# Input projection of a hybrid trunk: 28 column pairs over all tokens by seven block products, in a stage ahead of the mixers

## The chip, the cores and the metric

The kernel runs on one core of a Trainium2 chip. The metric is device time in microseconds (us) of one launch. The engines are TensorE (PE; PEld is its weight load), VectorE (DVE), ScalarE (ACT), GpSimd (POOL) and SyncE (SP), which here only issues DMAs.

## What is computed

One layer over 1024 tokens of width 1024, all in float32:

```python
h = layer_norm(x)
u = h @ w_in          # columns: conformer a, g | ssm z | ssm x, B, C | dt | gate_a | gate_b
y_a = silu(layer_norm(causal_dwconv31(a * sigmoid(g)))) @ w_conv_out
xbc = silu(causal_dwconv4([x, B, C]))
y_b = rms_norm(ssd(xbc, dt) * silu(z)) @ w_ssm_out     # chunks of 128 tokens, 4 groups, 32 heads
h = layer_norm(alpha * h + (sigmoid(gate_a) * y_a + sigmoid(gate_b) * y_b) @ w_o)
h = layer_norm(alpha * h + conv_ffn(h))               # 2 x 2816 columns up, 3-tap convolution, down
```

## The kernel before

Every float32 product is made of three products of float32r operands (hi by hi, hi by lo, lo by hi: lines 166, 167 and 168 of `mm3`); ScalarE rounds an operand to its high part, VectorE subtracts to get the low one. Activations lie by channels: a tile is 128 channels by 512 tokens, and tokens are taken in two halves of 512.

The program runs half 0 through `ln_in`, `mixers`, `combine` and `out_proj`, then half 1 through the same with `out_proj_pairs` at the end, then the FFN over both halves.

- `mixers` goes over four SSD groups. For each, `column` computes one 128-column tile of `w_in` (24 products of 512 columns: 8 blocks of the contraction by 3) for B, C and four tiles of x, and `conv4` filters each with 4 taps. `z_gate` computes the group's z. `glu` computes two tiles of a and of g; `conv31` filters them with 31 taps, 30 of them as one step on VectorE each (line 420), at a priority 1500 below the rest. `ssd_group` then works through four chunks of 128 tokens. After the groups come the eight columns of gate_a. From group 2 on `ssm_out_first` multiplies the first half of the SSD output with `w_so`.
- A chunk of `ssd_group` goes round the engines: GpSimd builds `au`, TensorE multiplies it with `seg_st` (line 487), ScalarE makes the decay (495, 496), VectorE multiplies with the masked scores `cbm` (512), TensorE multiplies with `xs` (534), VectorE adds up `t` (535). Most of these tiles have one buffer, and the chunks share four PSUM banks.
- `combine` computes the eight columns of gate_b, each followed by the rest of the SSD output (`w_sp`), and beside them the LayerNorm over channels of the convolved tiles (`cc`: GpSimd sums them, TensorE spreads the mean, lines 616 to 636); then `w_co` multiplies the result `sT`.
- The FFN's up projection takes columns in 22 pairs over all tokens. With the contraction, the columns and the tokens each cut in two, a pair is a product of 2x2 blocks, done with seven block products (84 products of 512 columns) in place of eight. `ffn_blocks` makes the sums of activation blocks (b11, b21, b22, t1 to t4), `up_weights` those of weights, `up_rest` adds the products up. For the first 8 pairs (`LEAD`) `up_first` computes two of the products ahead and stores them.

The order of instructions on each engine comes from a list scheduler that builds the program by the order of the code and priorities (`tc.high_priority(offset=...)`, negative for late); each engine then runs its list strictly in order. All DMAs are issued by SyncE, in order as well. `big` is a pool of two 32 KB-per-partition buffers for `hT`, `yT` and `mixT`; `wst` and `wsp` hold three weight tiles each.

```python
                with tc.high_priority(offset=-1500):
                    conv31(pl, hh, vs)
```

Of the kernel before, what the change touches and what calls it, by code (L numbers as in the profile page):

```python
# [8 lines left out]
F32 = mybir.dt.float32  # L9
# [7 lines left out]
P = 128  # L17
# [34 lines left out]
CT_A, CT_G, CT_X, CT_B, CT_C, CT_DT, CT_GA, CT_GB = 0, 8, 16, 32, 36, 40, 41, 49  # L52
CT_N = 57
# [3 lines left out]
def kernel(  # L57
# [3 lines left out]
    wcol: bass.AP,  # L61
# [33 lines left out]
    state_stack = ExitStack()  # L95
    statep = state_stack.enter_context(pool("states", side="right"))
    upper = statep.tile([P, P], F32, name="upper")
    make_upper_triangular(nc, upper, 1.0, diag=True)
    later = statep.tile([P, P], F32, name="later")
    make_lower_triangular(nc, later, 1.0, diag=False)  # L100
    ones = statep.tile([P, P], F32, name="ones")
    V.memset(ones, 1.0)
# [22 lines left out]
    a_log = statep.tile([P, HEADS], F32, name="a_log")  # L125
    dskip = statep.tile([P, HEADS], F32, name="dskip")
    u_halo = statep.tile([P, 24, 3], F32, name="u_halo")
    G.memset(u_halo, 0.0)
    v_halo = statep.tile([P, 8, KC - 1], F32, name="v_halo")
    G.memset(v_halo, 0.0)  # L130
    states = [statep.tile([P, HALF], F32, name=f"state{g}") for g in range(GROUPS)]
    dts = [statep.tile([P, 4, HEADS], F32, name=n) for n in ("dtv", "wds")]
    edc = statep.tile([P, 3, 4, HEADS], F32, name="edc")
    seg_mv = statep.tile([P, 4, P], F32, name="seg_mv")
    seg_st = statep.tile([P, 4, P], F32R, name="seg_st")
# [10 lines left out]
    g_scr = [dram.tile([8, P, HALF], F32, name=f"g_scr{i}") for i in range(2)]  # L146
# [87 lines left out]
    def ln_in(hh):  # L234
        hT = big_tile(f"hT{hh}")
        with pool(f"lnin{hh}", side="right") as pl:
            first = hh == 0
            xts, gb = [], []
            with tc.high_priority(offset=6000):
                for t in range(4):  # L240
                    xt = pl.tile([P, D], F32, tag="x", bufs=4, name=f"x{hh}_{t}")
                    r0 = hh * HALF + t * P
                    SY.dma_start(xt, x[r0 : r0 + P, :])
                    xts.append(xt)
                    if first and t == 1:
                        gb = [row(pl, RW_ING, D, "in_g"), row(pl, RW_INB, D, "in_b")]
            if not first:
                gb = [row(pl, RW_ING, D, "in_g"), row(pl, RW_INB, D, "in_b")]
            if first:
                SY.dma_start(pc[:, :PC_N], pcol)  # L250
                SY.dma_start(a_log, prow[RW_AL : RW_AL + HEADS].partition_broadcast(P))
                SY.dma_start(dskip, prow[RW_SD : RW_SD + HEADS].partition_broadcast(P))
            for t, xt in enumerate(xts):
                with tc.high_priority(offset=(6000 - 1000 * (t // 2)) if first else 0):
                    mv, rs = ln_stats(pl, [xt], f"in{hh}_{t}")
                    ln_apply(xt, mv, rs, 0, *gb)
                    SY.dma_start(h_scr[hh][t * P : (t + 1) * P, :], xt)
                    transpose_to(hT, xt, t, 0, KD)
        return hT
# [83 lines left out]
    def column(hh, hT, ct):  # L343
        ps = bank(1)
        project(ps, weights(wcol[ct], f"c{hh}_{ct}"), hT)
        return ps

    def first_columns(hh, hT, cts):

        ws = [weights(wcol[ct], f"c{hh}_{ct}", eng=None if hh else G) for ct in cts]  # L350
        pss = [bank(1) for _ in cts]
        for q in range(2):
            ts = slice(q * 256, (q + 1) * 256)
            for w, ps in zip(ws, pss):
                for n, (i, j) in enumerate(((0, 0), (1, 0), (0, 1))):
                    for k in range(KD):
                        TE.matmul(
                            ps[:, ts],
                            w[:, i, k * P : (k + 1) * P],
                            hT[:, j, k, ts],  # L360
                            start=n == 0 and k == 0,
                            stop=n == 2 and k == KD - 1,
                        )
        return pss

    def conv4(pl, hh, ps, j):

        u = pl.tile([P, HALF + 3], F32, tag="u", bufs=3, name=f"u{hh}_{j}")
        o = pl.tile([P, HALF], F32, tag="xbc", bufs=12, name=f"xbc{hh}_{j}")
        wc = PC_SW + j * 4  # L370
        A.copy(u[:, 3:], ps)
        A.copy(u[:, :3], u_halo[:, j, :])
        A.activation(out=o, in_=ps, func=AF.Identity, scale=pc[:, wc + 3 : wc + 4])  # L373
        for k in range(3):
            V.scalar_tensor_tensor(  # L375
                out=o,
                in0=u[:, k : k + HALF],
                scalar=pc[:, wc + k : wc + k + 1],
                in1=o,
                op0=ALU.mult,  # L380
                op1=ALU.add,
            )
        if hh == 0:
            A.copy(u_halo[:, j, :], u[:, HALF : HALF + 3])
        A.activation(out=o, in_=o, func=AF.Silu, bias=pc[:, PC_SB + j : PC_SB + j + 1])
        return o

    def glu(pl, hh, hT, i):
        pa, pg = bank(1), bank(1)
        wa = weights(wcol[CT_A + i], f"ga{hh}_{i}")  # L390
        project(pa, wa, hT)
        wg = weights(wcol[CT_G + i], f"gg{hh}_{i}")
        project(pg, wg, hT)
        v = pl.tile([P, HALF + KC - 1], F32, tag="v", bufs=4, name=f"v{hh}_{i}")
        s = pl.tile([P, HALF], F32, tag="sig", name=f"sig{hh}_{i}")
        A.activation(out=s, in_=pg, func=AF.Sigmoid)
        A.copy(v[:, : KC - 1], v_halo[:, i, :])
        V.tensor_mul(v[:, KC - 1 :], pa, s)
        if hh == 0:
            A.copy(v_halo[:, i, :], v[:, HALF:])  # L400
        return v

    def conv31(pl, hh, vs):

        accs = {}
        for i, v in vs:
            wc = PC_CW + i * KC
            c = pl.tile([P, HALF], F32, tag="c", bufs=2, name=f"c{hh}_{i}")
            A.activation(  # L409
                out=c,  # L410
                in_=v[:, KC - 1 :],
                func=AF.Identity,
                scale=pc[:, wc + KC - 1 : wc + KC],
                bias=pc[:, PC_CB + i : PC_CB + i + 1],
            )
            accs[i] = c
        for k in range(KC - 1):
            for i, v in vs:
                wc = PC_CW + i * KC
                V.scalar_tensor_tensor(  # L420
                    out=accs[i],
                    in0=v[:, k : k + HALF],
                    scalar=pc[:, wc + k : wc + k + 1],
                    in1=accs[i],
                    op0=ALU.mult,
                    op1=ALU.add,
                )
        for i, _ in vs:
            SY.dma_start(c_scr[hh][i], accs[i])
# [130 lines left out]
    def mixers(hh, hT):  # L560
        pre = first_columns(hh, hT, (CT_DT, CT_B, CT_C))
        with pool(f"mixers{hh}") as pl:
            time_steps(pl, hh, pre[0])
            for g in range(GROUPS):
                BT = conv4(pl, hh, column(hh, hT, CT_B + g) if g else pre[1], 16 + g)
                CT = conv4(pl, hh, column(hh, hT, CT_C + g) if g else pre[2], 20 + g)
                xT = [
                    conv4(pl, hh, column(hh, hT, CT_X + 4 * g + i), 4 * g + i) for i in range(4)
                ]
                zs = z_gate(pl, hh, hT, g)  # L570
                vs = [(i, glu(pl, hh, hT, i)) for i in (2 * g, 2 * g + 1)]
                done = ssd_group(pl, hh, g, xT, BT, CT, zs)
                if g == 2:
                    ssm_out_first(pl, hh, yT)
                if g % 2 == 0:
                    yT = big_tile(f"yT{hh}_{g}")
                done(yT)
                with tc.high_priority(offset=-1500):
                    conv31(pl, hh, vs)
            for j in range(8):  # L580
                pg = bank(1)
                project(pg, weights(wcol[CT_GA + j], f"gt{hh}_{j}"), hT)
                ga = pl.tile([P, HALF], F32, tag="ya", bufs=2, name=f"gt{hh}_{j}")
                A.activation(out=ga, in_=pg, func=AF.Sigmoid)
                SY.dma_start(g_scr[hh][j], ga)
        return yT
# [625 lines left out]
```

## Time and profile before

| | us |
|---|---|
| median of 3 runs | 2045.84 (2041.03 to 2046.99) |
| span of the profiled execution | 2043.0 |
| TensorE busy | 1977.0 (97%) |
| VectorE busy | 1717.1 (84%) |
| ScalarE busy | 1001.3 (49%) |
| GpSimd busy | 146.8 (7%) |

The profile is of one execution. It has groups of instructions (count, busy time, mean), a table of busy time by windows of the span, the instructions in order of time, and the chain of waits that ended last. Starts and lengths are in us from the span's start. Busy TensorE is the union of records that overlap (a product's record is about 0.4 us long, and one starts every 0.225), so its share says that it was never without work, not how fast it was.

By the rows in order of time, in half 0 the products with `w_so` start at 297, gate_a at 442, gate_b at 499, `w_co` at 598 and `w_o` at 642 us; half 1 starts at 691; the FFN's first products start at 1356, its pairs at 1413, and the down projection at 1805.

### The profile page before, as it was taken

How to read it: one execution, taken by the hardware profiler on the slowest of the kernel's cores; microseconds unless marked ns; L12 is line 12 of the kernel's file. 1: busy time of each engine (PE TensorE's matmuls, PEld its weight loads, DVE VectorE, ACT ScalarE, POOL GpSimd, SP SyncE). 2: the span in 40 equal slices, each digit the busy share in tenths (PEclk: the TensorE clock that was granted, in tenths of full speed). 3: DMA queues.
4: the chain of work that ended last, by engine and by line, in shares of the span. 5: the costliest groups of instructions: out<-in, count | busy, mean ns of one | idle time of the engine just before them, and what ended most of it. 6: DMA issues, size and time to landing. Idle time of an engine off the chain costs nothing. (4 is left out here: it accounts for less than half of the span.)

```text
span 2043.0 us, 24683 instructions
## 1 busy us (share of the span) xinstructions
PE 1977.0 (97%) x9164; PEld 1627.7 (80%) x9164; DVE 1717.1 (84%) x2279; ACT 1001.3 (49%) x1431; POOL 146.8 (7%) x125
## 2 busy tenths in 40 slices
PE   7999999999999999999999999997899999989998
PEld 6888887888788888888888888876678888768886
DVE  7599999989766859999998976596888788789668
ACT  4465654556452356665454645453334445444432
POOL 2010101000400001010100040010000000000000
PEclk9999999999999999999999999998989999999999
DMA  6212223223436522222323253564343223287463
GB/s 218 93 68 89 87 93 103 98 103 114 160 124 218 200 93 73 93 78 87 117 88 109 107 175 127 207 234 174 124 138 119 95 98 117 101 316 267 145 226 109
DMA packets 99192, 275.10 MB, mean 135 GB/s; under 512 B 11264, under 2 KB 11264, under 8 KB 99072
## 3 DMA queue, kind: packets, MB, share of 16 engines
q1 hardware_dynamic: 99072, 273.52, 38.4%
q8 instruction: 72, 1.18, 0.2%
q14 instruction: 48, 0.39, 0.1%
HBM read 223.93 MB, written 49.55 MB: 134 GB/s over the span
## 5 line engine op out<-in xcount | busy, mean ns | idle before, releaser
L420 DVE SCALAR_TENSOR_TENSOR c<-v,pc,c 128x512 f32<-128x512 f32 x480 | 374.5, 803 | 7.7 <-ACT c L409 6.4
L478 POOL TENSOR_TENSOR au<-seg_mv,head_of 128x1024 fp32r<-128x1024 f32 x32 | 76.4, 2386 | 963.0 <-PE sm L487 730.1
L166 PE MATMUL acc<-hT,w_c 128*128 128x512 f32 x352 | 141.0, 401 | 0.0
L167 PE MATMUL acc<-hT,w_c 128*128 128x512 f32 x352 | 140.6, 399 | 0.0
L168 PE MATMUL acc<-hT,w_c 128*128 128x512 f32 x352 | 138.4, 393 | 0.0
L375 DVE SCALAR_TENSOR_TENSOR xbc<-u,pc,xbc 128x512 f32<-128x512 f32 x144 | 109.6, 773 | 0.7 <-ACT xbc L373 0.5
L1006 ACT CAST w_dn<-dr 128x1024 fp32r<-128x1024 f32 (+1 forms) x73 | 68.3, 944 | 76.6 <-PE sm L168 27.4
L167 PE MATMUL acc<-w_z,hT 128*128 128x512 f32 x256 | 100.8, 394 | 0.0
L166 PE MATMUL acc<-w_z,hT 128*128 128x512 f32 x256 | 100.8, 401 | 0.0
L168 PE MATMUL acc<-w_z,hT 128*128 128x512 f32 x256 | 100.7, 396 | 0.0
L154 ACT CAST w_c<-st_c 128x1024 fp32r<-128x1024 f32 x50 | 52.6, 1051 | 86.9 <-PE acc L168 66.2
L1007 DVE TENSOR_TENSOR w_dn<-dr,w_dn 128x1024 fp32r<-128x1024 f32 (+1 forms) x73 | 78.6, 1086 | 9.3 <-ACT w_dn L1006 9.1
L167 PEld LDWEIGHTS acc<-hT,w_c 128*128 128x128 f32 x352 | 66.1, 188 | 16.9 <-issue 3.8
L168 PEld LDWEIGHTS acc<-hT,w_c 128*128 128x128 f32 x352 | 66.1, 188 | 16.1 <-issue 2.6
L166 PEld LDWEIGHTS acc<-hT,w_c 128*128 128x128 f32 x352 | 66.1, 188 | 16.0 <-issue 2.6
L155 DVE TENSOR_TENSOR w_c<-st_c,w_c 128x1024 fp32r<-128x1024 f32 x47 | 60.5, 1287 | 20.3 <-ACT w_c L154 20.3
L166 PE MATMUL acc<-h1b,w_ue 128*128 128x512 f32 x176 | 68.8, 391 | 2.6 <-ACT w_ue L731 1.4
L731 ACT CAST w_s<-rb 128x1024 fp32r<-128x1024 f32 x22 | 23.2, 1053 | 94.7 <-PE sm L168 73.1
L166 PE MATMUL sm<-h1b,w_s 128*128 128x512 f32 x176 | 69.4, 395 | 0.0
L167 PE MATMUL sm<-h1b,w_s 128*128 128x512 f32 x176 | 69.2, 393 | 0.0
L168 PE MATMUL sm<-h1b,w_s 128*128 128x512 f32 x176 | 69.0, 392 | 0.0
L167 PE MATMUL acc<-h1b,w_ue 128*128 128x512 f32 x176 | 68.5, 389 | 0.0
(348 smaller groups left out, 5859.7 us busy)
## 6 DMA issues: line engine op xcount, KB each, us to landing
st_c<-wcol SPq DMA_DIRECT2D x50, 512.0 KB, 3.5
st_z<-wz SPq DMA_DIRECT2D x32, 512.0 KB, 3.5
dr<-wdown SPq DMA_DIRECT2D x55, 256.0 KB, 4.4
st_wo<-wo SPq DMA_DIRECT2D x24, 512.0 KB, 4.1
ra<-wup SPq DMA_DIRECT2D x22, 512.0 KB, 3.5
rb<-wup SPq DMA_DIRECT2D x22, 512.0 KB, 3.5
t_scr<-fo SPq DMA_DIRECT2D x22, 512.0 KB, 4.3
dr<-t_scr SPq DMA_DIRECT2D x44, 256.0 KB, 3.2
```

The source lines that it names most:

```text
L154: A.copy(w[:, 0, :], st)
L155: (eng or V).tensor_tensor(out=w[:, 1, :], in0=st, in1=w[:, 0, :].bitcast(F32), op=ALU.subtract)
L166: TE.matmul(ps, wa(0), xa(0), start=start, stop=False, skip_group_check=more)
L167: TE.matmul(ps, wa(0), xa(1), start=False, stop=False, skip_group_check=more)
L168: TE.matmul(ps, wa(1), xa(0), start=False, stop=stop, skip_group_check=more)
L375: V.scalar_tensor_tensor(out=o, in0=u[:, k : k + HALF], scalar=pc[:, wc + k : wc + k + 1], in1=o, op0=ALU.mult, op1=ALU.add,)
L420: V.scalar_tensor_tensor(out=accs[i], in0=v[:, k : k + HALF], scalar=pc[:, wc + k : wc + k + 1], in1=accs[i], op0=ALU.mult, op1=ALU.add,)
L478: G.tensor_tensor(out=au, in0=seg_mv[:, c, :].unsqueeze(1).to_broadcast([P, 8, P]), in1=head_of[:, g, :].unsqueeze(2).to_broadcast([P, 8, P]),
L731: A.copy(w[:, 0, :], src)
L1006: A.copy(w[:, 0, cs], src)
L1007: V.tensor_tensor(out=w[:, 1, cs], in0=src, in1=w[:, 0, cs].bitcast(F32), op=ALU.subtract)
```

## The change

All columns of `w_in` but z and dt are computed ahead of the mixers, over all 1024 tokens, in 28 pairs by the same seven block products as in the FFN: 8 pairs of a and g, 12 pairs of B, C and x tiles, 8 pairs of gate_a and gate_b. The FFN's functions become general ones (`Blocks`, `pair_first`, `pair_weights`, `pair`) that both stages call. The results (v after the GLU, the filtered and activated `xbc` tiles, the two gates after the sigmoid) are stored to DRAM, and the mixers and `combine` load the half that they need. `conv31` becomes a function of one tile and one half: the eight of half 0 stand among the pairs at a priority 1200 below, the eight of half 1 ahead of the first mixers at 1500 below. z is still computed in the mixers, from `bl.b1` for half 0 and from tiles that `second_half` transposes for half 1. In `pair` two copies into PSUM replace sums on VectorE. Stores of v, c, h and of the FFN's tiles are issued by GpSimd, those of the leads, `xbc` and the gates by ScalarE. `sT` takes a buffer of `big`.

```diff
-    hT = ln_in(0)
-    yT = mixers(0, hT)
-    mixT = combine(0, hT, yT)
-    hT = ln_in(1)
+    blocks_stack = ExitStack()
+    qp = blocks_stack.enter_context(pool("inq", side="right"))
+    with pool("inputs") as tp:
+        bl = input_blocks(tp, qp)
+    with pool("leads", side="right") as fp:
+        for j in range(LEAD):
+            pair_first(fp, bl, win[2 * j], lead_scr[j], f"i{j}")
+    conv_stack = ExitStack()
+    convp = conv_stack.enter_context(pool("conv"))
+    with pool("in") as upp:
+        for n in range(PAIRS_GLU + PAIRS_CONV + PAIRS_GATE):
+            in_pair(upp, bl, n)
+            if n >= PAIRS_GLU and n % 2 == 0 and n < PAIRS_GLU + 16:
+                with tc.high_priority(offset=-1200):
+                    conv31(convp, 0, (n - PAIRS_GLU) // 2)
+    blocks_stack.close()
...
+    with tc.high_priority(offset=-1500):
+        for i in range(8):
+            conv31(convp, 1, i)
+    yT = mixers(0, bl.b1)
+    mixT = combine(0, yT)
+    hT = second_half()
...
+    def conv31(pl, hh, i):
+        v = pl.tile([P, HALF + KC - 1], F32, tag="v", bufs=2, name=f"v{hh}_{i}")
+        c = pl.tile([P, HALF], F32, tag="c", bufs=2, name=f"c{hh}_{i}")
...
+            SY.dma_start(v, v_scr[i][:, HALF - KC + 1 :])
...
+        G.dma_start(c_scr[hh][i], c)
...
     def mixers(hh, hT):
-        pre = first_columns(hh, hT, (CT_DT, CT_B, CT_C))
...
-                BT = conv4(pl, hh, column(hh, hT, CT_B + g) if g else pre[1], 16 + g)
...
+                def part(j):
+                    o = pl.tile([P, HALF], F32, tag="xbc", bufs=12, name=f"xbc{hh}_{j}")
+                    SY.dma_start(o, xbc_scr[j][:, hh * HALF : (hh + 1) * HALF])
+                    return o
...
-                vs = [(i, glu(pl, hh, hT, i)) for i in (2 * g, 2 * g + 1)]
...
-                with tc.high_priority(offset=-1500):
-                    conv31(pl, hh, vs)
-            for j in range(8):
-                pg = bank(1)
-                project(pg, weights(wcol[CT_GA + j], f"gt{hh}_{j}"), hT)
...
     def combine(hh, hT, yT):
-                project(pg, weights(wcol[CT_GB + j], f"gb{hh}_{j}"), hT)
+                SY.dma_start(gb, gb_scr[j][:, ht])
...
+    def pair(upp, bl, w1, w2, scr, nm, pad):
...
+        ps, pz = bank(1), bank(0)
         if ue:
+            product(ps, lambda i: ue[:, i, :HALF], bl.of("b11"), True)
             py = bank(1)
+            A.copy(py, ps)
         else:
+            SY.dma_start(s, scr[0])
+            SY.dma_start(ug[:, early], scr[1])
+            A.copy(ps, s)
+        product(pz, lambda i: w3[:, i], bl.of("t3"), True)
+        product(ps, lambda i: w24[:, i, :HALF], bl.of("t2"), False)
+        A.copy(s, ps)
+        if ue:
+            product(py, lambda i: ue[:, i, HALF:], bl.of("b21"), False)
+            A.copy(ug[:, early], py)
+        product(ps, lambda i: w10[:, i, :HALF], bl.of("t1"), False)
+        A.copy(uv[:, late], ps)
+        V.tensor_tensor(out=uv[:, late], in0=pz, in1=uv[:, late], op=ALU.subtract)
+        product(pz, lambda i: w10[:, i, HALF:], bl.of("t4"), False)
+        V.tensor_tensor(out=uv[:, early], in0=pz, in1=s, op=ALU.subtract)
+        product(ps, lambda i: w24[:, i, HALF:], bl.of("b22"), False)
+        A.copy(ug[:, late], ps)
+        return ug, uv
```

How the lists of instructions change, at three places. First VectorE, where it splits `w_so_4`, the fifth weight tile of the SSD output of half 0. The kernel before has there (`c_3`, `c_4`: convolution tiles of half 0; `m_2_0`: chunk 0 of group 2):

```order
L420 SCALAR_TENSOR_TENSOR c_4_3084<-v_4_2508,pc,c_4_3084 128x512
L512 TENSOR_TENSOR m_2_0_2593<-m_2_0_2593,cbm_2_0_2602 128x1024
L420 SCALAR_TENSOR_TENSOR c_3_2016<-v_3_1769,pc,c_3_2016 128x512
L155 TENSOR_TENSOR w_so_3_2886<-st_so_3_2884,w_so_3_2886 128x1024
L420 SCALAR_TENSOR_TENSOR c_4_3084<-v_4_2508,pc,c_4_3084 128x512
L420 SCALAR_TENSOR_TENSOR c_3_2016<-v_3_1769,pc,c_3_2016 128x512
L155 TENSOR_TENSOR w_so_4_2919<-st_so_4_2917,w_so_4_2919 128x1024
```

and the changed kernel (`c_6` and `c_7` are the last two tiles of half 1):

```order
L424 TENSOR_TENSOR m_2_0_5751<-m_2_0_5751,cbm_2_0_5760 128x1024
L333 SCALAR_TENSOR_TENSOR c_6_4677<-v_6_4676,pc,c_6_4677 128x512
L140 TENSOR_TENSOR w_so_3_6044<-st_so_3_6042,w_so_3_6044 128x1024
L333 SCALAR_TENSOR_TENSOR c_7_4712<-v_7_4711,pc,c_7_4712 128x512
L333 SCALAR_TENSOR_TENSOR c_6_4677<-v_6_4676,pc,c_6_4677 128x512
L140 TENSOR_TENSOR w_so_4_6077<-st_so_4_6075,w_so_4_6077 128x1024
```

At the same point of the work, VectorE's list before has some steps of the fourth and fifth convolution tile of 16; the new one has finished fourteen tiles and stands in the last two.

Second TensorE, at the last chunk of group 3 of half 0. Before (`w_gb`: gate_b, `w_sp`: rest of the SSD output):

```order
L168 MATMUL acc_4223<-hT_184,w_gb_0_4226 128x512
L166 MATMUL acc_4257<-yT_2_3049,w_sp_0_4260 128x512
L534 MATMUL sm_3842<-xs_3_3_3824,m_3_3_3813 128x64 x8
L167 MATMUL acc_4257<-yT_2_3049,w_sp_0_4260 128x512
L168 MATMUL acc_4257<-yT_2_3049,w_sp_0_4260 128x512
```

and now:

```order
L388 MATMUL sm_6540<-xbc_23_6244,xbc_19_6242 128x128
L399 MATMUL sm_6546<-au_3_3_6543,seg_st 128x512
L399 MATMUL sm_6550<-au_3_3_6543,seg_st 128x512
L427 MATMUL sm_6565<-state_4460,xbc_23_6244 128x512
L435 MATMUL sm_6570<-xsd_3_3_6560,bt_3_3_6562 128x512
L446 MATMUL sm_6574<-xs_3_3_6556,m_3_3_6545 128x64 x8
L177 MATMUL sm_6590<-ident,t_3_0_6408 128x128 x4
```

The columns of the gates stood between a chunk's products; now chunks 2 and 3 of the group stand there with nothing between them.

Third GpSimd, in the mixers of half 0. Before:

```order
L478 TENSOR_TENSOR au_0_3_1130<-seg_mv,head_of 128x1024
L478 TENSOR_TENSOR au_1_0_1786<-seg_mv,head_of 128x1024
L478 TENSOR_TENSOR au_1_1_1832<-seg_mv,head_of 128x1024
L478 TENSOR_TENSOR au_1_2_1884<-seg_mv,head_of 128x1024
L478 TENSOR_TENSOR au_1_3_1936<-seg_mv,head_of 128x1024
```

and now:

```order
L390 TENSOR_TENSOR au_1_0_5370<-seg_mv,head_of 128x1024
L341 DMA c_scr_151<-c_4_4607 128x512
L390 TENSOR_TENSOR au_1_1_5416<-seg_mv,head_of 128x1024
L341 DMA c_scr_151<-c_5_4642 128x512
L390 TENSOR_TENSOR au_1_2_5468<-seg_mv,head_of 128x1024
L390 TENSOR_TENSOR au_1_3_5520<-seg_mv,head_of 128x1024
```

The stores of finished convolution tiles of half 1 moved into GpSimd's list, between the chunks' `au`.

478 lines of the change are left out of this document (222 added, 256 removed).

## Prediction

> **What bounds the kernel now.** I read the page's header and chain first, then the table of 50 us windows (below the column line), then the groups of VectorE.
>
> ```profile
> span 2043.0 us, 24683 instructions
> PE 1977.0 (97%) x9164; PEld 1627.7 (80%) x9164; DVE 1717.1 (84%) x2279; ACT 1001.3 (49%) x1431; POOL 146.8 (7%) x125
> PE 25%; DVE 3%; DMA 2%; issue 1%; ACT 0%; SPq 0%; DVEq 0%; ACTq 0%
> ...
> core 0: us, PE busy (x) PEld busy (x) DVE busy (x) ACT busy (x) POOL busy (x), PEclk, DMA share, GB/s
> 0.00:50.00 50.00, 35.34 (x227) 32.15 (x228) 38.43 (x63) 22.79 (x44) 10.87 (x15) 1.00 0.63 222
> 200.00:250.00 50.00, 50.00 (x243) 40.94 (x241) 50.00 (x70) 33.98 (x61) 6.86 (x3) 1.00 0.23 79
> 600.00:650.00 50.00, 50.00 (x222) 41.39 (x221) 26.07 (x34) 14.73 (x18) 0.00 (x0) 1.00 0.47 149
> 1400.00:1450.00 50.00, 36.77 (x149) 28.89 (x150) 33.78 (x46) 14.49 (x17) 0.20 (x2) 0.90 0.38 137
> 1450.00:1500.00 50.00, 44.83 (x186) 36.35 (x185) 46.03 (x56) 18.14 (x18) 0.60 (x6) 0.93 0.41 137
> 1500.00:1550.00 50.00, 45.50 (x190) 37.07 (x189) 45.21 (x55) 18.76 (x19) 0.60 (x6) 0.93 0.40 143
> ```
>
> TensorE sets the time: 97% busy. But in the mixers (200 to 250) VectorE is just as full: 50.00 of 50, beside a TensorE that never stops. The scheduler filled every gap of VectorE there with steps of the 31-tap convolution. VectorE has air in the combine stage (26.07 of 50). So a change that takes work from TensorE and gives some to VectorE must be judged by where the VectorE work stands, not by TensorE's sum.
>
> One product 128x128 by 512 columns takes 50/222 = 0.225 us of TensorE. Slots of VectorE (start to next start, since neighbours overlap by 0.07) are read from rows in time order (the one without operands is from the chain of waits); two groups stand below them:
>
> ```profile
> 203.04 1.41 DVE L420 SCALAR_TENSOR_TENSOR c<-v,pc,c 128x512 f32<-128x512 f32 x2
> 204.37 0.68 DVE L500 TENSOR_TENSOR xs<-sm,dtv 128x512 f32<-128x512 f32 x1
> 204.97 0.68 DVE L504 TENSOR_TENSOR t<-sm,dskip 128x512 f32<-128x512 f32 x1
> ...
> 1446.97 1.20 DVE fo L898
> 1464.36 1.22 DVE L732 TENSOR_TENSOR w_s<-rb,w_s 128x1024 fp32r<-128x1024 f32 x1
> 1465.50 0.68 DVE L912 TENSOR_TENSOR fo<-fo,fo 128x512 f32<-128x512 f32 x1
> ...
> L420 DVE SCALAR_TENSOR_TENSOR c<-v,pc,c 128x512 f32<-128x512 f32 x480 | 374.5, 803 | 7.7 <-ACT c L409 6.4
> L375 DVE SCALAR_TENSOR_TENSOR xbc<-u,pc,xbc 128x512 f32<-128x512 f32 x144 | 109.6, 773 | 0.7 <-ACT xbc L373 0.5
> ```
>
> A tap over 512 columns: (204.37 - 203.04)/2 = 0.665 us; a two-operand step over 512: 0.60; over 1024: 1.14; a tap over 1024: 1.20.
>
> **The change, part by part.** *TensorE.* 56 column tiles by 2 token halves by 24 products were 2688; 28 pairs by 84 are 2352. 336 fewer by 0.225 is -75.7 us.
>
> *VectorE.* Splits of weights: 110 of 1.14 go, 98 come (-14). Four sums of weights per pair: 112 by 0.60 (+67). Two differences per pair on the way out: 56 by 0.60 (+34). The 4-tap convolution: 144 by 0.665 become 72 by 1.20 (-9). The block sums of the input and the second transposition: 36 more of 0.60 (+22). Altogether about +100 us.
>
> *ScalarE and the queues.* ScalarE has 150 copies of 512 columns more and 28 casts of 1024 fewer:
>
> ```profile
> L371 ACT COPY u<-acc 128x512 f32<-128x512 f32 x48 | 27.7, 577 | 0.0
> L154 ACT CAST w_z<-st_z 128x1024 fp32r<-128x1024 f32 x32 | 33.6, 1049 | 33.3 <-PE acc L168 33.1
> ...
> st_c<-wcol SPq DMA_DIRECT2D x50, 512.0 KB, 3.5
> c_scr<-c SPq DMA_DIRECT2D x16, 256.0 KB, 2.7
> ```
>
> 150 by 0.58 less 28 by 1.05 is +58 us on an engine at 49%: nothing alone. Of DMA, 48 weight loads of 512 KB go, and v, the 24 filtered tiles and both gates are stored and read again; at a mean of 135 GB/s in the page nothing waits for bandwidth. What is new is who issues: the stores of v, c and the FFN's tiles leave SyncE's queue for GpSimd's, where the store of a finished convolution tile stands ahead of the au products of the next chunks. Such a store waits for the last of 30 low-priority steps, and so does the SSD chunk behind it. SyncE's loads of v for later convolutions likewise stand ahead of loads of SSD inputs. I price both at nothing, since VectorE's order puts the same steps ahead of the same chunks; if that cover goes, each is a landing of 2.7 to 3.5 us, once per convolution tile of the second half (28 us in all at most).
>
> *Where VectorE's work stands.* This decides. In the order of the changed program, I count what VectorE has to do ahead of its split of w_so_4, the fifth weight tile of the SSD output in the first half: 476 steps of 0.665 (466 of them of the 31-tap convolution; the kernel before has 123 there), 321 of 0.60, 119 of 1.14, 88 of 1.20, and about 20 us of small ones: 317 + 193 + 136 + 106 + 20 = 770 us. Group L420's mean of 803 ns against 773 in L375 tells that some steps run slower beside GpSimd; with 0.06 more on each it is 798. I take 780, nearer the lower end since most of the steps now stand where GpSimd computes nothing. VectorE's idle time ahead of it is at least 50 - 38.43 = 12 us (the start). It may be 45, since the first eight rows now come through three buffers and their blocks need all of LayerNorm before product b11 can start; I take 20. So w_so_4 is split at about 800 us (782 to 843).
>
> *TensorE behind that point.* Its first product with w_so_4 is followed by 4716 products of 512 columns and 23 SSD chunks. In the kernel before, the piece from the first product with w_sp (first half) has 6036 and 17:
>
> ```profile
> 505.50 0.39 PE L166 MATMUL acc<-yT,w_sp 128*128 128x512 f32 x1
> ...
> 125.10 0.40 PE L487 MATMUL sm<-au,seg_st 128*128 128x512 f32 x1
> 125.53 0.60 ACT L495 ACTIVATE m<-sm 128x512 f32<-128x512 f32 x1
> 128.88 1.28 ACT L496 ACT_TABLE_LOAD   x1
> 129.61 1.02 PE L523 MATMUL sm<-xsd,bt 128*128 128x512 f32 x2
> 133.02 1.21 DVE L512 TENSOR_TENSOR m<-m,cbm 128x1024 f32<-128x1024 f32 x1
> 136.40 1.89 PE L534 MATMUL sm<-xs,m 128*128 128x64 f32 x16
> 138.82 0.47 PE L487 MATMUL sm<-au,seg_st 128*128 128x512 f32 x1
> ```
>
> That piece lasted 2043.0 - 505.5 = 1537.5 us with all its waits. 1320 fewer products are -297; 6 more chunks by about 5.3 us (1.89 for L534, 1.02 for L523, as much for L515, the rest small) are +32: 1272 us. 800 + 1272 = 2072.
>
> *FFN.* Two copies into PSUM replace VectorE's sums: 3 by 0.60 in each of the 8 lead pairs is 14 us off an engine that had 46.03 and 45.21 of 50 while TensorE stood still for 13.2 + 5.2 + 4.5 = 23 us (1400 to 1550). I take -10 (ends: -23, and +5 if the stores, now issued by GpSimd, land later). The 14 others are TensorE's.
>
> *Gates gone from the middle.* The columns gate_a and gate_b were TensorE's cover while the last group's chunks ran and while the convolution's LayerNorm was computed. In the order of the changed program, 4.4 columns of w_sp (24 us) stand between the product that gives the mean and the first one with w_co. The trace has this for the chain that must end first:
>
> ```profile
> 542.10 4.87 DVE L623 TENSOR_TENSOR cc<-cc,sm 128x512 f32<-128x512 f32 x8 [1.52 <-PE sm L620]
> 575.29 0.82 ACT L637 ACTIVATE cc<-cc,pc 128x512 f32<-128x512 f32 x1
> ```
>
> From 542 to 576 and a split: 35 us, 11 more than the cover; w_co's first products need only the first tiles of it, so I take 7 us of stall in each half (0 to 12): +14. And the last two chunks of a group of four stand alone on TensorE. The steps of a chunk in series (0.4 + 0.6 + 1.28 + 0.6 + 1.21 + 1.89 + 0.68) come to 6.7 us; in the trace the loop takes 138.82 - 125.10 = 13.7 with queues. I take 9 against 5.3 of products, for three chunks a half, and the norm's transposition behind them: 12 us a half, +24 (0 to 60).
>
> The sum: 2072 - 10 + 14 + 24 = 2100, against the profiled execution's 2043.0. The median of the runs, 2045.84, lies 2.8 above that span; rounded within the error, **2100 us**, 2.7% slower.
>
> **Rivals.** *Faster: all low ends together.* 770 + 12 + 1272 - 23 = 2031, with 2.8: 2034. It needs a VectorE that never waits for anything in 780 us; for it speaks that it did so in 200 to 250. The plain reading of the sum (2043 - 76 - 10 + 3 = 1960) would need the 466 convolution steps to be elsewhere than the order puts them. Chance 0.10 for both. The point that decides: VectorE's total ahead of w_so_4 would have to be under 765 us.
>
> *No change.* As above with 12 us of idle time or stalls more: 2040 to 2052. Chance 0.07.
>
> *Slower still: the chunks keep the pace of before.* Two neighbouring chunks in the trace stand 13.7 to 19 us apart; mixers(1) needs 576 products by 0.225 and 16 chunks by 5.3, or 13.4 us a chunk. At 16 us a chunk it adds 16 x 2.6 = 42 us: 2142; at 19, 90 us. For it: the loop goes through four engines and buffers that exist once. Against: the pace of before was set by the other work in the queues. Chance 0.14.
>
> *The clock.* After a long gap TensorE comes back slowly:
>
> ```profile
> 1405.00:1415.00 10.00, 2.11 (x5) 1.74 (x6) 7.08 (x11) 3.21 (x4) 0.00 (x0) 0.57 0.70 269
> 1415.00:1425.00 10.00, 10.00 (x41) 8.17 (x41) 9.55 (x15) 1.67 (x2) 0.00 (x0) 0.91 0.49 157
> 1495.00:1505.00 10.00, 10.00 (x46) 8.28 (x45) 9.87 (x14) 2.11 (x2) 0.10 (x1) 1.00 0.49 164
> 1445.00:1455.00 10.00, 9.18 (x39) 7.32 (x40) 9.95 (x13) 5.04 (x5) 0.10 (x1) 1.00 0.39 122
> ```
>
> A gap of some 8 us left a granted clock of 0.57 and then 0.91, and 41 products where 46 fit (1.1 us lost in that window); a window with short gaps kept 1.00. With stalls of 4 us in every chunk of both mixers, 2 us each, of which only those behind w_so_4 count (some 20), this is +40: 2140. Chance 0.08. The Trainium skill (TensorE: Matmul & The Clock Gate, section Part 1: The HAM clock gate) says that an idle window of about 3.4 us halves the clock until some 3.4 us of work have passed; the trace agrees with 0.57 after the long gap and with 1.00 after short ones. By that rule, an estimate from the page, each gap over the window costs about 1.7 us, and 20 of them 34: 2134.
>
> **How the numbers follow.** Forecast 0.61 (its own range 2055 to 2125), paced chunks 0.14, clock 0.08, no change 0.07, faster 0.10. Within 0.3% (2040 to 2052) is about what a measurement here can tell from no change. The range 2040 to 2145 leaves out the faster case and the upper part of the paced one. Faster 0.10, same 0.07, slower 0.83.
>
> **What the profile after would show.** TensorE's count falls by 336 of its 9164 or a few more. VectorE's busy time rises to about 1800 us. Windows of the first 550 us: VectorE near 50 of 50 and TensorE at 45 to 48. Between 600 and 800 us: VectorE full with group c<-v,pc,c, TensorE half idle, its granted clock under 1.00, its waits ended by VectorE. From mixers(1) on VectorE far from full. The lead pairs of the FFN: TensorE back to about 48 of 50. I am wrong if TensorE is above 90% busy in the first 800 us, or if the first product with w_so_4 comes before 770 us; and if it comes at 800 but the rest lasts under 1240 us, then the piece behind is mis-sized.

## Result and profile after

The changed kernel takes 2212.78 us (median of 4 runs, 2210.4 to 2214.85), the kernel before 2044.5 on the same chip: ratio 1.082, 95% interval 1.0801 to 1.0839. The forecast was 2100; the time lies above its range. First lines of the page of the changed kernel:

```profile
span 2208.7 us, 24089 instructions
PE 1990.7 (90%) x8716; PEld 1597.8 (72%) x8716; DVE 1794.3 (81%) x2368; ACT 996.4 (45%) x1383; POOL 169.0 (8%) x228
PE 64%; DVE 18%; issue 7%; DMA 6%; ACT 5%; POOL 0%; DVEq 0%; SPq 0%; ACTq 0%; POOLq 0%
```

TensorE has 448 fewer records and is busy 14 us longer: 90% in place of 97%. The chain has 18% of VectorE. (The 3% of the kernel before can't be set beside it: the chain there is followed back only to 1400 us, 31% of the span.) The rows in order of time give the stages (start, length, engine):

```profile
31.98 1.22 PE L151 MATMUL acc<-h0b,w_pei 128*128 128x512 f32 x2
...
601.15 0.39 PE L151 MATMUL acc<-h0b,w_dt 128*128 128x512 f32 x1
...
841.26 1.22 DVE L140 TENSOR_TENSOR w_so<-st_so,w_so 128x1024 fp32r<-128x1024 f32 x1
...
1052.81 0.39 PE L151 MATMUL acc<-w_wo,mixT 128*128 128x512 f32 x1
...
1098.09 0.39 PE L151 MATMUL acc<-hT,w_dt 128*128 128x512 f32 x1
...
1486.22 0.39 PE L151 MATMUL acc<-w_wo,mixT 128*128 128x512 f32 x1
```

The stage lasts until the first product with dt (601), where its 2352 products need 2352 x 0.226 = 532 us. From there to the first product with `w_o` half 0 takes 452 us and half 1 takes 388. What is left in a half is 984 products (221 us) and 16 chunks of about 5.3, 306 us. So 69, 146 and 82 us are lost (some 8 in each half are the norm's 64 transpositions and the time steps, which both kernels have). The kernel before was busy in 592 of 597 us of half 0 and all but 1 us of half 1:

```profile
45.00:642.00 597.00, 592.20 (x2772) 485.94 (x2771) 514.60 (x697) 321.98 (x495) 60.88 (x30) 1.00 0.31 105
691.00:1305.00 614.00, 613.05 (x2941) 506.29 (x2940) 534.22 (x730) 326.70 (x482) 61.00 (x30) 1.00 0.32 109
```

The table of windows of the changed kernel shows who was busy (columns, as in the two rows above: busy PE, PEld, DVE, ACT, POOL with counts, granted clock, DMA share, GB/s; the sum row runs from 0 to 841.3):

```profile
0.00:50.00 50.00, 23.80 (x109) 19.65 (x110) 44.12 (x74) 21.80 (x41) 4.57 (x13) 1.00 0.70 247
250.00:300.00 50.00, 49.55 (x218) 40.25 (x217) 50.00 (x62) 27.67 (x33) 0.50 (x5) 1.00 0.27 96
601.00:1053.00 452.00, 368.28 (x1581) 286.95 (x1580) 378.49 (x533) 176.75 (x272) 61.27 (x42) 0.86 0.32 107
650.00:700.00 50.00, 28.88 (x113) 22.30 (x111) 48.42 (x78) 11.18 (x20) 6.51 (x5) 0.70 0.17 56
1098.00:1486.00 388.00, 337.09 (x1524) 265.97 (x1523) 258.87 (x354) 170.36 (x262) 53.20 (x30) 0.91 0.32 107
1160.00:1200.00 40.00, 27.58 (x111) 20.22 (x110) 20.74 (x27) 17.43 (x28) 5.68 (x3) 0.83 0.12 40
sum 841.30, PE 727.47 PEld 576.35 DVE 784.54 ACT 386.89 POOL 41.72; mean PE 60.62 PEld 48.03 DVE 65.38 ACT 32.24 POOL 3.48
```

In the first mixers (650 to 700) VectorE is full and TensorE half idle, as forecast. TensorE's waits there do not end as forecast, though: from 601 to 841 the waits that end on ScalarE come to 35 us, those on VectorE to 22. In the second mixers (1160 to 1200) TensorE has gaps although VectorE, with all 31-tap steps done, is only half busy. This is what a chunk looks like there, in the rows of TensorE and ScalarE:

```profile
1171.01 0.75 PE L399 MATMUL sm<-au,seg_st 128*128 128x512 f32 x2
1171.53 1.09 ACT L407 ACTIVATE m<-sm 128x512 f32<-128x512 f32 x2 [7.92 <-PE sm L399]
1172.63 1.28 ACT L408 ACT_TABLE_LOAD   x1
1173.92 1.15 ACT L408 ACTIVATE m<-m 128x512 f32<-128x512 f32 x2
1174.98 0.61 ACT L450 ACTIVATE sq<-t 128x512 f32<-128x512 f32 x1
1175.50 0.19 ACT L450 ACTIVATION_READ_ACCUMULATOR sq<-t 128x1 f32 x1
1175.70 1.28 ACT L360 ACT_TABLE_LOAD   x1
1177.00 0.60 ACT L360 ACTIVATE zs<-acc 128x512 f32<-128x512 f32 x1
1177.65 0.79 PE L151 MATMUL acc<-w_z,hT 128*128 128x512 f32 x1 [4.35 <-ACT zs L360]
1178.24 0.63 PE L152 MATMUL acc<-w_z,hT 128*128 128x512 f32 x1
...
1182.08 0.48 PE L152 MATMUL acc<-w_z,hT 128*128 128x512 f32 x1
1182.40 0.40 PE L153 MATMUL acc<-w_z,hT 128*128 128x512 f32 x1
```

The z products of the next group need PSUM banks that ScalarE's silu (L360) empties. In ScalarE's list that silu stands behind the chunk's decay and two table loads, so TensorE waits 4.35 us in the middle of a chunk. Then its products start 0.43 us apart, not 0.23, for 4.4 us: some 2 us more. Of half 1's 82 us TensorE is idle for 51; in the other 31 it is busy beyond the price of its products, at a mean granted clock of 0.91. None of its waits there ends on a DMA, so nothing points to the loads of `xbc` and the gates.

### The profile page after: what moved, and what is told of

Read it like the earlier page. It is cut to its first block, busy times and chain, and to the rows that moved or that the text cites. A ratio compares the mean times of both kernels' runs of the same rounds, so it can differ in the third digit from the quotient of the medians.

```text
span 2208.7 us, 24089 instructions
## 1 busy us (share of the span) xinstructions
PE 1990.7 (90%) x8716; PEld 1597.8 (72%) x8716; DVE 1794.3 (81%) x2368; ACT 996.4 (45%) x1383; POOL 169.0 (8%) x228
## 4 chain that ended last, share of the span: by engine, by line
PE 64%; DVE 18%; issue 7%; DMA 6%; ACT 5%; POOL 0%; DVEq 0%; SPq 0%; ACTq 0%; POOLq 0%
PE acc L151 16%; PE acc L153 15%; PE acc L152 15%; DVE c L333 5%; PE sm L153 4%; PE sm L151 4%; PE sm L152 4%; PE sm L446 3%; DVE foc L831 1%; PE sm L435 1%; DVE w_s_i L637 1%; DMA su<-first_scr 1%; DMA c_scr<-c 1%; DVE t L448 1%; DMA c<-wdown 1%
## 5 line engine op out<-in xcount | busy, mean ns | idle before, releaser
L333 DVE SCALAR_TENSOR_TENSOR c<-v,pc,c 128x512 f32<-128x512 f32 x480 | 359.6, 783 | 7.3 <-ACT c L325 6.8
L151 PE MATMUL acc<-h0s,w_s_i 128*128 128x512 f32 x336 | 134.3, 400 | 14.2 <-ACT acc L806 7.7
L153 PE MATMUL acc<-h0s,w_s_i 128*128 128x512 f32 x336 | 131.2, 390 | 0.0
L152 PE MATMUL acc<-h0s,w_s_i 128*128 128x512 f32 x336 | 130.9, 390 | 0.0
L407 ACT ACTIVATE m<-sm 128x512 f32<-128x512 f32 x64 | 36.3, 594 | 175.8 <-PE sm L399 175.6
L151 PE MATMUL acc<-h1s,w_s_u 128*128 128x512 f32 x264 | 104.8, 398 | 8.0 <-ACT acc L806 7.6
L152 PE MATMUL acc<-h1s,w_s_u 128*128 128x512 f32 x264 | 103.4, 392 | 0.0
L153 PE MATMUL acc<-h1s,w_s_u 128*128 128x512 f32 x264 | 103.4, 392 | 0.0
L446 PEld LDWEIGHTS sm<-xs,m 128*128 128x128 f32 x512 | 73.9, 224 | 24.6 <-issue 19.0
L151 PEld LDWEIGHTS acc<-h0s,w_s_i 128*128 128x128 f32 x336 | 63.0, 188 | 38.6 <-ACT si L809 12.1
L151 PE MATMUL sm<-h0b,w_s_i 128*128 128x512 f32 x224 | 87.8, 392 | 1.9 <-ACT w_s_i L636 1.9
L979 DVE TENSOR_TENSOR w_dn<-dr,w_dn 128x1024 fp32r<-128x1024 f32 (+1 forms) x73 | 78.5, 1088 | 13.0 <-ACT w_dn L978 12.8
L152 PE MATMUL sm<-h0b,w_s_i 128*128 128x512 f32 x224 | 87.8, 392 | 0.0
L153 PE MATMUL sm<-h0b,w_s_i 128*128 128x512 f32 x224 | 86.7, 393 | 0.0
L446 PE MATMUL sm<-xs,m 128*128 128x64 f32 x512 | 73.5, 306 | 10.6 <-DVE m L424 10.5
L153 PEld LDWEIGHTS acc<-h0s,w_s_i 128*128 128x128 f32 x336 | 63.1, 188 | 13.7
L152 PEld LDWEIGHTS acc<-h0s,w_s_i 128*128 128x128 f32 x336 | 63.1, 188 | 12.3
L151 PE MATMUL acc<-w_dn 128*128 128x512 f32 x160 | 59.0, 396 | 12.3 <-ACT w_dn L978 12.3
L151 PE MATMUL sm<-h1b,w_s_u 128*128 128x512 f32 x176 | 68.3, 390 | 1.7 <-ACT w_s_u L636 1.7
L152 PE MATMUL sm<-h1b,w_s_u 128*128 128x512 f32 x176 | 68.5, 389 | 0.0
```

The source lines that it names most:

```text
L151: TE.matmul(ps, wa(0), xa(0), start=start, stop=False, skip_group_check=more)
L152: TE.matmul(ps, wa(0), xa(1), start=False, stop=False, skip_group_check=more)
L153: TE.matmul(ps, wa(1), xa(0), start=False, stop=stop, skip_group_check=more)
L333: V.scalar_tensor_tensor(out=c, in0=v[:, k : k + HALF], scalar=pc[:, wc + k : wc + k + 1], in1=c, op0=ALU.mult, op1=ALU.add,)
L407: A.activation(out=mq, in_=pg, func=AF.Relu)
L446: TE.matmul(py[:, hs], m[:, h, :], xs[:, hs], start=True, stop=True)
```

## Experiments

All times are medians, each ratio is to the kernel before on the same chip. "A half" is from the first product with dt to the first with `w_o`. Three theories: LIST (VectorE's list sets the time of the first mixers, the forecast's step), COVER with LOOP (a chunk's round trip over the engines is exposed, since the columns between its steps are gone), CLOCK.

**1. Half 1's taps left out.**

```diff
-        for k in range(KC - 1):
+        for k in () if hh == 1 else range(KC - 1):
```

> Leaves out 30 of the 31 taps of the convolution for the eight tiles of half 1 (240 VectorE steps); everything else as in the changed kernel. Theory LIST (the step on which the forecast rests: VectorE's list ahead of w_so_4 sets the time of the first mixers): with 226 fewer steps ahead of it, the split of w_so_4 of half 0 comes at 770 to 790 us in place of 841, since mixers(0) then lasts as long as mixers(1), 244 us from z to w_sp in place of 294; the whole falls by 50 to 70 us, to 2143 to 2163. Rival COVER (the chunk loop of the SSD sets the pace, because the projection columns that stood between its steps on TensorE are gone): chunks keep 15 to 17 us in half 0, and the whole falls by at most 25 us, 2188 to 2213.

Measured 2172.44 us (1.0623, 1.0594 to 1.0652), 40 less. In its profile (span 2160.7 us) `w_so_4` is split at 793.53, half 0 falls from 452 to 405 us, half 1 stays (390). Some 160 us of VectorE's work are worth 40 by the medians: the figure lies between the two expectations, and the split is nearer to LIST's 770 to 790.

**2. All taps left out**, the same edit for both halves.

> Leaves out 30 of the 31 taps of the convolution in both halves (all 480 VectorE steps). The run without those of half 1 stood at 2172 us, its first dt product still at 600. LIST: the stage too is slowed by VectorE (50 of 50 busy from 250 to 600 us), so it falls from 600 to 560 us (532 of products and some 26 lost at the start): 2125 to 2140. Rival: the stage's loss is the start and the waits between a pair's own steps, VectorE's spare steps only fill it: the first dt product stays at 590 to 600, and the whole at 2160 to 2175. In both the chunks keep 15 to 16 us in half 0 by LOOP.

Measured 2158.94 us (1.0556, 1.053 to 1.0583). The first dt product comes at 594: the rival holds for the stage, whose loss is its own. VectorE's split in this kernel:

```profile
787.46 1.23 DVE L140 TENSOR_TENSOR w_so<-st_so,w_so 128x1024 fp32r<-128x1024 f32 x1 [0.63 <-ACT w_so L139]
```

and its window:

```profile
600.00:790.00 190.00, 156.32 (x703) 121.55 (x701) 107.44 (x158) 87.15 (x133) 21.32 (x14) 0.88 0.27 91
```

Without one step of the convolution, VectorE is busy 107 of 190 us and `w_so_4` is still split at 787. Taking away all of the convolution's steps gives back 54 us of the 168 lost, and the kernel before has these steps too.

**3. Half 1's convolution in mixers(1).**

```diff
                 done(yT)
+                if hh == 1:
+                    with tc.high_priority(offset=-1500):
+                        for i in (2 * g, 2 * g + 1):
+                            conv31(pl, 1, i)
...
-    with tc.high_priority(offset=-1500):
-        for i in range(8):
-            conv31(convp, 1, i)
     yT = mixers(0, bl.b1)
...
```

> The eight convolutions of half 1 stand in mixers(1), two behind each group, at the same priority 1500 below, with their tiles in its pool, so that none can run before. LIST: half 0 gains the same 50 to 70 us (w_so_4 split at 770 to 790), and mixers(1), whose VectorE has about 19 of 50 us free, gets 240 steps by 0.7 = 168 us for about 110 us of room: it gets 40 to 60 us longer; whole 2190 to 2215. COVER: the pace of the chunks is the loop's own; half 0 gains under 25 us and half 1 loses little: 2195 to 2215. The two differ in where w_so_4 of half 0 is split: under 800 by LIST, over 815 by COVER.

Measured 2250.51 us (1.1012, 1.0993 to 1.1031), slower than either expected; `w_so_4` is split at 790, as LIST said. Half 0 gains as in run 1 (406 us), half 1 grows from 388 to 468. 41 of these 80 us lie between the first products with `w_sp` and `w_co` (133 us where it was 92): the last tile is stored late, and only then can GpSimd sum the tiles for the mean:

```profile
1429.97 0.54 POOL L341 DMA_DIRECT2D c_scr<-c  x1 [1.66 <-DVE c L333]
1430.52 1.27 POOL L525 TENSOR_TENSOR mean<-cc,cc 128x512 f32<-128x512 f32 x1
```

**4. Gates by halves again**, as 16 columns a half in the mixers and in combine.

> The 16 gate columns are computed by halves again, gate_a behind the groups of the mixers and gate_b in combine, as in the kernel before; 20 pairs stay in the stage. 96 products more (+22 us). The scheduler then puts 349 convolution steps ahead of the split of w_so_4 in place of 466. COVER: from w_sp to w_co nothing is lost any more (33 and 30 us lost in the changed kernel) and the last chunks of each half are covered by gate_a (some 20 us each): 2213 + 22 - 63 - 40 = 2130, with the shorter list down to 2080. LIST alone, without any worth in the cover: the split of w_so_4 comes at about 700, 768 products by 0.225 more stand behind it: 700 + 1367 + 173 = 2240 less nothing, so 2200 to 2240.

Measured 2192.06 us (1.0729, 1.0713 to 1.0745). The stage falls to 448; half 0 takes 528 and half 1 445, with 393 us of products: 135 and 52 lost. The gates' cover is worth 11 and 30 us, far less than COVER's 100; most of it lies behind the chunks. LIST's floor of 2200 was missed too.

**5. Only the a and g pairs ahead**, x, B and C by halves as well.

> Of the 28 pairs only the eight of a and g stay in the stage; the columns of x, B, C and both gates are computed by halves in the mixers and in combine, as in the kernel before. By products, a half then holds 306 us of the changed kernel's mixers and combine plus 40 columns by 5.4, 523 us; the stage of eight pairs lasts about 221 us (448 with 20 pairs, less 12 by 18.9). COVER (the columns of x, B and C fill TensorE between the steps of the chunks): a half loses at most 15 us beyond its products, where the changed kernel loses 146 and 82: 221 + 538 + 47 + 538 + 724 = 2068, at most 2090. LIST without cover: the losses of the run with the gates by halves stay, 135 and 52: 2225.

Measured 2111.35 us (1.0326, 1.0303 to 1.0349). Windows of this kernel: half 0, half 1, and two within half 0:

```profile
207.00:807.00 600.00, 558.95 (x2511) 448.01 (x2510) 583.35 (x814) 297.11 (x470) 65.19 (x54) 0.95 0.32 104
854.00:1385.00 531.00, 527.36 (x2487) 432.20 (x2486) 373.26 (x493) 290.42 (x437) 55.15 (x32) 1.00 0.33 108
400.00:500.00 100.00, 76.65 (x311) 57.05 (x310) 94.41 (x142) 46.37 (x73) 11.19 (x8) 0.78 0.13 45
500.00:600.00 100.00, 100.00 (x481) 82.17 (x480) 100.00 (x137) 49.39 (x86) 7.22 (x5) 1.00 0.37 118
```

Half 1 needs 523 us by its products and takes 531, with TensorE busy in 527: with the columns of x, B and C back between the chunks' steps, 8 us are lost where 82 were (52 with the gates alone, run 4). COVER is shown for half 1. Its 2068 was missed by half 0, which still loses 77 us with VectorE nearly full.

**6. The same, with half 1's convolution in mixers(1).**

> As the run with only the a and g pairs ahead, but the eight convolutions of half 1 stand in mixers(1). LIST (in that run VectorE had 188 of 200 us in 300 to 500 and 98 of 100 behind it, and half 0 lost 77 us): without the 150 or so steps of half 1 ahead of its end, half 0 loses 10 to 25, and half 1, where VectorE has some 170 us free for 168 us of steps, loses 20 to 40 in place of 8: 2111 - 60 + 20 = 2071 (2055 to 2085). LOOP (half 0's loss is the chunks' round trip): half 0 still loses 60 or more, whole 2105 to 2140.

Measured 2150.17 us (1.0521, 1.0504 to 1.0538), slower than run 5 where LIST expected faster, and 10 above LOOP's range. Half 0 gains only 12 us (588, still 65 lost, as LOOP said), half 1 loses 51 (582). The step that fell: I had put half 0's loss to half 1's steps. The list has 185 steps of half 0 ahead of `w_so_0` in both kernels (the kernel before: 103). I put that to all eight tiles being ready at once, which was not tested. Two windows of this kernel, half 0 and half 1:

```profile
400.00:500.00 100.00, 77.59 (x329) 58.85 (x328) 93.83 (x141) 47.32 (x74) 11.35 (x9) 0.78 0.16 54
...
1050.00:1150.00 100.00, 71.84 (x321) 55.08 (x320) 97.05 (x143) 38.93 (x63) 12.09 (x9) 0.80 0.19 59
```

**7. Chunks staggered** (on the changed kernel).

```diff
+        ready = [front(0)]
+        for c in range(4):
+            if c < 3:
+                ready.append(front(c + 1))
+            back(c, *ready[c])
```

> In ssd_group the front of chunk c+1 (transpositions, scores, decay, m) is written ahead of the back of chunk c (products with state, xsd and m), with two buffers for m, xs, xsd and bt; nothing else changes. Theory LOOP (the loss in the mixers is TensorE's wait for the round of one chunk through ScalarE and VectorE, one after the other in the lists): with the next front in between, the waits shrink; half 1, whose VectorE is not full, loses 30 to 50 in place of 82 us, half 0 gains 10 to 30: 2130 to 2170. If the waits came from VectorE's total alone (LIST), half 1 gains nothing and the whole stays within 15 us of 2213.

Measured 2163.46 us (1.0581, 1.0558 to 1.0603), within LOOP's range. Half 0 gains 20 (432), half 1 gains 31 (357), and its chunks come every 12.8 us in place of 15.3. TensorE's waits in half 1, of the changed kernel (the three largest) and of this one (the largest, and the one on `zs`):

```profile
PE acc L151 <- ACT zs L360: 20.0, 5, 4.3
PE sm L177 <- DVE t L456: 11.0, 3, 5.7
PE sm L446 <- DVE m L424: 6.0, 2, 3.2
```

```profile
PE sm L177 <- DVE t L471: 17.3, 2, 9.9
...
PE acc L151 <- ACT zs L360: 3.0, 3, 1.3
```

The wait on `zs` nearly goes; the wait at the end of a group, where TensorE transposes the normed `t`, grows from 11.0 to 17.3 us.

**8. Buffers of a chunk doubled.**

> au, m, xs and xsd of a chunk get two buffers; the lists of all engines keep their order. BUFFERS (the forecast's rival that named buffers that exist once): the chunks of half 1 come every 11 to 13 us in place of 15.3, whole 2150 to 2180. LOOP (the lists run in order, so the next chunk can't start earlier whatever buffers there are): within 10 us of 2213.

Measured 2215.38 us (1.0833, 1.081 to 1.0857): nothing, as LOOP said. The lists run in order, and a second buffer lets no instruction past another. The PSUM banks, `bt` and `cbm` stayed as they were, so the rival falls for these four tiles only.

**9. Staggered, half 1's taps left out.**

> Staggered chunks, and 30 of 31 taps of the convolution of half 1 left out. If LIST and LOOP are two limits that lie side by side in mixers(0) (VectorE's sum and the chunks' round), taking both away gives more than the 49 and 40 us apart: half 0 goes from 432 (staggered) to about 360, as half 1 does, whole 2163 - 70 = 2093 (2085 to 2108). If they simply add up: 2163 - 40 = 2123. If the stagger had relieved VectorE's order alone, no more than 2150.

Measured 2100.42 us (1.0275, 1.0259 to 1.029). Half 0 takes 367 us, nearly half 1's 357. Apart the two edits gave 49 and 40 us, together 112; in half 0 alone, by the profiles, 20 and 47, together 85. That is two limits of nearly the same height side by side. Window of half 0:

```profile
603.00:970.00 367.00, 337.00 (x1581) 269.98 (x1580) 245.45 (x339) 168.10 (x264) 53.33 (x34) 0.95 0.36 121
```

**10. Run 6 with staggered chunks.**

> The run before last with staggered chunks (xbc tiles in 10 buffers, since 12 do not fit beside them). COVER: with the columns between the chunks' steps the round trip is hidden anyway: within 15 us of the kernel without stagger. LOOP as a loss of its own: 30 to 50 us less than that kernel.

Measured 2131.16 us (1.0423, 1.0406 to 1.0439), 19 less than run 6: between the two expectations. Half 0 gains 6 us and half 1 gains 10. Cover hides the round trip for the most part. What is left may lie where VectorE is full (94 and 97 of 100 us in run 6's two windows); that was not tested.

**11. Ten idle products a chunk.**

```diff
             py = bank(0)
+            for k in range(10):
+                TE.matmul(py, hT[:, 0, k % 8, :P], hT[:, 0, k % 8, :], start=True, stop=True)
```

> Each of the 32 chunks gets ten products of 512 columns that nobody uses, written ahead of the eight products with m into the same bank, where TensorE waits for m. 320 by 0.225 = 72 us of TensorE. Theory CLOCK (the low granted clock of 0.70 to 0.89 in the mixers lengthens the chunk's own products, which stand at 3.5 us in place of 1.89 in the last chunks): the clock in the mixers rises above 0.95 and the whole falls by 20 to 50 us, to 2163 to 2193. COVER and LIST (TensorE waits there for the other engines): the clock rises, the time stays within 15 us of 2213, and the 72 us go into the waits. If TensorE were the bound there, 2285.

Measured 2209.3 us (1.0816, 1.0791 to 1.084), equal to the changed kernel. Three windows of this kernel (the changed kernel's granted clock in them is 0.83, 0.80 and 0.70):

```profile
1160.00:1200.00 40.00, 38.32 (x190) 30.04 (x188) 22.57 (x32) 22.66 (x34) 5.78 (x3) 1.00 0.25 79
1220.00:1260.00 40.00, 32.04 (x157) 25.88 (x156) 24.99 (x38) 20.75 (x33) 5.50 (x3) 0.83 0.14 47
1360.00:1400.00 40.00, 30.93 (x143) 23.98 (x144) 27.51 (x36) 12.68 (x26) 12.76 (x9) 0.83 0.22 73
```

In the first of them the granted clock rises to 1.00, and TensorE, with the idle products, from 27.58 to 38.32 of 40 us. Elsewhere it rises less: over the whole of half 0 from 0.86 to 0.92, over half 1 from 0.91 to 0.95, so CLOCK's condition (above 0.95) was met in part only. The 72 us of products vanish in the waits: TensorE's sum of work does not set the time there. CLOCK's 20 to 50 us did not come. Whether a warmer clock gives something that the idle products take back, this run can't tell, so what the clock alone is worth stays open.

**12. The kernel before with the new FFN pair alone.**

```diff
-            A.copy(s, ps)
             py = bank(1)
-            product(py, lambda i: ue[:, i, HALF:], bl["b21"], True)
-            V.tensor_tensor(out=ug[:, early], in0=s, in1=py, op=ALU.add)
...
+            A.copy(py, ps)
...
+            product(py, lambda i: ue[:, i, HALF:], bl["b21"], False)
+            A.copy(ug[:, early], py)
```

> The kernel before with one part of the change alone: the pairs of the FFN as the change writes them (two copies into PSUM in place of sums on VectorE, the order of its block products, stores issued by GpSimd and ScalarE). In the changed kernel the FFN lasts 672.4 us from its first product, before 687.2. The forecast's term (-10, ends -23 and +5) and the trace both say a gain here: 2044 - 15 = 2029 (2021 to 2037). Rival: the gain comes from the emptier queues ahead of it in the changed kernel; then within 5 us of 2044.

Measured 2029.44 us against 2044.88 (0.9932, 0.9918 to 0.9946), as expected: this part of the change is worth 15 us by itself, and the kernel beats both others. Its windows where TensorE's busy time was 36.77, 44.83 and 45.50:

```profile
1400.00:1450.00 50.00, 45.71 (x195) 36.10 (x196) 35.46 (x44) 24.63 (x32) 1.02 (x4) 1.00 0.43 140
1450.00:1500.00 50.00, 45.77 (x199) 36.88 (x198) 45.75 (x54) 26.24 (x34) 4.35 (x13) 1.00 0.50 165
1500.00:1550.00 50.00, 47.78 (x210) 38.91 (x209) 42.22 (x48) 25.43 (x31) 3.39 (x12) 1.00 0.33 111
```

## Why the prediction was right and wrong

*Right: the direction, and the products.* 336 products of 512 columns go; the other 112 records are first columns that had been cut into products of 256, less new transpositions. VectorE rose by 77 us (forecast 100).

*Where VectorE's work stands: sum right, idle time wrong, and only half a cause.* VectorE is busy 784.54 us up to the split of `w_so_4`; I took 780. Its idle time is 57 us, not 20, so the split stands at 841 and not 800. I looked for that idle time at the start, with 45 us as a bound. It is not there: VectorE is busy 44.12 of the first 50 us (38.43 before). 28 us of it lie between 50 and 150 us, in the lead pairs and the first pairs behind them (first half of that stretch in the row below), 13 of them waiting for ScalarE's casts of weights; 15 us lie behind 601. But the step's conclusion, that VectorE's total sets that moment, holds in part only: run 2 has it at 787 with those 466 steps gone. VectorE's sum without any idle time (784) and the chunks' round trip behind the stage (787) come within 3 us of each other, so a theory with one of them alone came near by luck. That the two take turns, and so give 841, is my reading; run 9 bears it out: only with both relieved does half 0 fall to near half 1's time.

```profile
50.00:100.00 50.00, 46.94 (x202) 37.81 (x201) 38.01 (x57) 26.72 (x44) 0.71 (x3) 0.97 0.68 230
```

*TensorE behind that point: mis-sized, the step that failed most.* Forecast 1272 - 10 + 14 + 24 = 1300, measured 2208.7 - 841.3 = 1367. I scaled a piece of the kernel before by its product count. That piece's chunks had columns between their steps, and in the term "Gates gone from the middle" I counted only three chunks a half as uncovered. In fact all 16 lost them: the columns of x, B and C went into the stage too, and z and the products with `w_so` alone don't fill a half. Half 1 alone lost 82 us, where the two terms had 19 a half: some 50 of them ahead of the first product with `w_sp` (249 us for 600 products and twelve chunks), for which I had no term, and some 28 between that and the first with `w_co` (92 us for 192 products and four chunks). The two steps, 41 us up to the split and 67 behind it, are nearly the whole of the 113 us that the forecast missed. Runs 5 and 7 name the cause from both sides: cover returned, 8 us lost; the loop shortened, 31 us gained. The rival "the chunks keep the pace of before" had the right mechanism at 0.14 (chunks came every 15.3 to 16.9 us, its price at 16 was +42); the buffers that exist once, which it also named, were not a reason as far as run 8 doubled them. None of the prediction's own signs of being wrong came up (TensorE was 87% busy in the first 800 us, the split came behind 770), and for a longer rest behind 800 it had no sign.

*The gates.* For the convolution's LayerNorm I took 7 us a half. The trace has 4.47 us of waiting in half 1 and 3.5 + 2.7 in half 0 (rows below): as taken. The gates as cover for the last chunks are worth 11 and 30 us (run 4).

```profile
1439.30 1.65 PE L151 MATMUL acc<-sT,w_co 128*128 128x512 f32 x3 [4.47 <-ACT sT L167]
```

Some waits of TensorE in half 0 of the changed kernel; the one on `au` is for the point on the queues below:

```profile
PE sm L399 <- POOL au L390: 7.0, 1, 7.0
...
PE acc L152 <- DVE sT L168: 3.5, 1, 3.5
PE acc L151 <- ACT sT L167: 2.7, 1, 2.7
```

*FFN.* -10 forecast, 687.2 - 672.4 = 14.8 measured, 15 alone (run 12).

*Queues at nothing.* GpSimd's stores of `c` stand between the chunks' `au`, and one wait of TensorE, of 7.0 us, ends on an `au` in half 0. That `au` did not wait for a store (the last one ahead of it was issued at 673 us) but for `seg_mv`, which VectorE wrote between steps of the convolution:

```profile
681.94 2.27 POOL L390 TENSOR_TENSOR au<-seg_mv,head_of 128x1024 fp32r<-128x1024 f32 x1 [8.29 <-DVE seg_mv L295]
```

So no wait of TensorE on a late store shows in the mixers, and the term at nothing holds as far as this trace goes. The stores were not moved by themselves.

*The clock.* The gap of 4.35 us above was followed by 4.4 us at half rate. The Trainium skill (TensorE: Matmul & The Clock Gate, section Part 1: The HAM clock gate) has 3.4 us of idle time and 3.4 us of half speed; the trace agrees, with a slightly longer cold time. By the rule alone, 20 such gaps would have made +34 us (an estimate from the page); run 11, with the clock warmer in part and 72 us of idle products added, took the same time, so the price of the cold clock by itself was not measured.

*Open.* The stage loses 69 us, of which 32 are the start and at most 7 VectorE's convolution steps (run 2); the other 30 stand in the lead pairs and the pairs behind them and were not taken apart by a run. In the trace TensorE is idle for 25 us between 32 and 601; the largest of these waits end on ScalarE's copies into PSUM (7.7 and 4.2 us, lines 806 and 802). PSUM banks, of which the chunks share four, were not varied. Of half 1's 82 us, the staggered kernel still loses 51.

## What to carry to other kernels

Work taken off the busiest engine is a gain only if it didn't fill the waits of a loop through several engines: before you move it, find that loop's round trip where nothing fills it, and count every turn of it that becomes bare. A busy total that equals the time to some point doesn't prove that it sets it; ask what the next limit is and where it lies. And a change of many parts should be timed in parts: the FFN's pair alone was worth 0.7%, and by the two ratios the rest of the change cost 8.9%.

## What the runs showed that I had not expected

Switching ScalarE's function costs 1.28 us of its list and nothing behind it: the table load at 1172.63 ends at 1173.91 and the next activation starts at 1173.92; in 52 of the 56 loads of this trace neither the instruction ahead nor the activation behind is more than 0.02 us away. Two of them stand in one chunk's round trip. 72 us of idle products, with the warmer clock that they bring, changed the time by nothing measurable. And moving the same 240 steps of VectorE from ahead of half 0 into half 1 cost 38 us where I expected nothing: half 0 gained 46, half 1 lost 80, about half of that because the last tile then came too late for the LayerNorm.
